# A Mamba-2 layer on one core: the scan's products and transposes in one insert per pair, x and z of a pair change places

## The chip, the core and the metric

The kernel runs on one core of a Trainium2 chip. The metric is the device time of one execution in microseconds (us). Before the change three runs took 1293.35, 1293.44 and 1298.07 us; the median is 1293.44 us.

## What is computed

One layer of a streaming encoder on 512 tokens with 2048 channels: RMSNorm, a Mamba-2 mixer, a residual add and a final RMSNorm, all in float32.

```
hn  = rmsnorm(x, ln_g)
proj = hn @ w_in                       # 2048 -> z 4096, x 4096, B 8*128, C 8*128, dt 64
xbc = silu(causal_depthwise_conv(x|B|C, 4 taps))
dt  = softplus(dt + dt_bias);  a = -exp(a_log)
y   = ssd_scan(xs * dt, dt * a, B, C)  # 64 heads of 64 channels, 8 groups share B and C, state 128
y   = y + d_skip * xs
y   = rmsnorm(y * silu(z), norm_g)
out = rmsnorm(x + y @ w_out, final_g)
```

## The kernel before

**Float32 from two halves.** Every weight tile is split into a rounded part `hi` (a CAST on ScalarE, ACT, line 87) and a rest `lo` (a subtraction on VectorE, DVE, line 88). A product is then three matmuls per 128x128 block: hi times x hi, hi times x lo, lo times x hi (lines 635 to 637).

**Stages.** After a short first part (B, C, x and z of the first two units, called plain) come 36 pairs, then the output projection. The 4096 inner channels are 32 units of 128 channels (two heads). A pair is the projection of two tiles of 128 channels: x and z of one unit, or, once per group of four units, B and C of the next group. The order of the pairs is x,z of unit 4g, of 4g+1, then B,C of group g+1, then x,z of 4g+2 and of 4g+3.

**A pair.** `pair` (line 639) computes both tiles with seven products in place of eight (a Strassen form over the two halves of the 2048 inputs and the two halves of the tokens). Each product is 24 matmuls, that is 4 steps of 6 matmuls, and a pair is 28 steps (`QS`). The products of a pair are R11 (steps 0 to 4), T1 (4 to 8), the previous pair's T4 (8 to 12), T2 (12 to 16), R22 (16 to 20), R21 (20 to 24) and T3 (24 to 28); a pair's own T4 is done in the next pair (`last`). PSUM tile `R` holds T1 and R22, `S` holds R11, T2 and T3, `mm` the sum that T4 ends. One of the two tiles (`zq`, lines 679 and 683) is complete when T3 is, at step 28; the other when T4 is, at step 40, which is step 12 of the next pair. Before the change x is the later one (line 398) and z the earlier one (line 689).

**The weights of a pair** come in four loads on SP's queue (line 81: `ra`, `rb`, two `rc`), T1 and T3 are made by accumulating DMAs on GpSimd (POOL, line 598), T2 and T4 by additions on DVE (line 604). `q_events` says at which step each is loaded, formed and split.

**The scan of a unit** is six functions, hung on steps after the start of the unit's pair by the table in line 713:

- `u_load`: three DMAs on SP, of which `csb` (line 440, 512 KB, one buffer) is the decay row spread over all partitions.
- `u_decay`: twelve ACT instructions (lines 456 to 458) and one more (459) that make the decay mask `m` from `csb`, and a DVE multiplication (461).
- `u_xt`: four transposes on TensorE (PE, line 473) of `xs`, the convolved x after its SiLU (line 394), then `xd` and `xw` on DVE.
- `u_state` (PE line 488, then the split `sts`) and `u_yd` (PE lines 502 and 506, then DVE 509).
- `u_yo`: three matmuls (lines 518 to 520), DVE 521 to 523, the store of y to `yscr` (SP, line 524), and the sum of squares (ACT 528, DVE 529).

A group also has `g_cb` (lines 433 and 434, the products of B and C) and `g_bt` (line 416, transposes of B).

**What sets the order.** PE, SP and POOL run their instructions in the order in which the program gives them: `run(step)` calls what the tables put on a step ahead of that step's matmuls. DVE and ACT get their order from a scheduler that works on priorities; `urgent()` raises one. All queues run in order: an instruction that waits holds up those behind it. SP runs ahead of PE until a transfer's buffer or data isn't there; the store of y is where it mostly stands.

Of the kernel before, what the change touches and what calls it, by code (L numbers as in the profile page):

```python
# [10 lines left out]
F32 = mybir.dt.float32  # L11
F32R = mybir.dt.float32r
AF = mybir.ActivationFunctionType
ALU = mybir.AluOpType
# [3 lines left out]
P = 128  # L18
L = 512
# [7 lines left out]
UPG = 4  # L27
NU = G * UPG
# [6 lines left out]
def mamba_layer(ctx: ExitStack, tc: tile.TileContext, d: dict, out: bass.AP):  # L35
    nc = tc.nc
    V, S, T, Q = nc.vector, nc.scalar, nc.tensor, nc.gpsimd
# [3 lines left out]
    urgent = tc.high_priority  # L41
# [9 lines left out]
    sp = ph1.enter_context(tc.tile_pool(name="ssd", bufs=1))  # L51
# [52 lines left out]
    yscr = [dram.tile([P, UPG, L], F32, name=f"yscr{g}") for g in range(G)]  # L104
# [4 lines left out]
    NPL = 8  # L109
    seq = [(("B", 0), ("C", 0))]  # L110
# [2 lines left out]
            seq.append((("B", u // UPG + 1), ("C", u // UPG + 1)))  # L113
        seq.append((("x", u), ("z", u)))
    plain = [s for pair in (seq[0], seq[1], seq[2], seq[3]) for s in pair]
    quads = seq[NPL // 2:]
    tile_of = {"z": 0, "x": 32, "B": 64, "C": 72}
    QS = 28
    at = {s: i * KT for i, s in enumerate(plain)}
# [49 lines left out]
    xr = sp.tile([P, L + 48], F32, name="xr")  # L169
# [15 lines left out]
    sx = const.tile([P, L], F32, name="sx")  # L185
# [94 lines left out]
    rbc = const.tile([P, L], F32, name="rbc")  # L280
# [104 lines left out]
    def conv_silu(t, name):  # L385

        ca = sp.tile([P, L], F32, name=name, bufs=2)
        V.tensor_scalar(out=ca, in0=xr[:, 3:L + 3], scalar1=convw[:, t, 3:4], scalar2=convb[:, t:t + 1],
                        op0=ALU.mult, op1=ALU.add)
        for k in range(3):  # L390
            V.scalar_tensor_tensor(out=ca, in0=xr[:, k:k + L], scalar=convw[:, t, k:k + 1], in1=ca,
                                   op0=ALU.mult, op1=ALU.add)
        with urgent():
            S.activation(ca, ca, AF.Silu)
        return ca

    def normed(ps):
        V.tensor_tensor(out=xr[:, 3:L + 3], in0=ps, in1=rbc, op=ALU.mult)  # L398
# [9 lines left out]
    un = [dict() for _ in range(NU)]  # L408

    def g_b(g):  # L410
        gr[g]["B"] = conv_silu(32 + g, "bc")
# [10 lines left out]
    def g_c(g):  # L422
        gr[g]["C"] = conv_silu(40 + g, "bc")
        gr[g]["Cs"] = split(gr[g]["C"][:, LH:L], [P, LH], "cst", 2)
# [70 lines left out]
    def u_yd(u):  # L495

        pyd = ps_yd.tile([P, 2, 2 * P], F32, name="yd")
        xs, x, m = un[u]["xs"], un[u]["xd"], un[u]["m"]
        for i in range(2):
            for hh in range(2):  # L500
                r = slice(hh * HD, hh * HD + HD)
                T.matmul(pyd[r, i, :], x[:, 2 * i, hh, :], m[:, i, hh::4, :],  # L502
                         start=i == 0, stop=False, skip_group_check=True)
            for hh in range(2):
                r = slice(hh * HD, hh * HD + HD)
                T.matmul(pyd[r, i, P:2 * P], x[:, 2 * i + 1, hh, :], m[:, i, 2 + hh, :],
                         start=False, stop=i == 1, skip_group_check=True)
        y = xs
        V.scalar_tensor_tensor(out=y, in0=xs, scalar=dskip[:, u:u + 1], in1=pyd.rearrange("p c l -> p (c l)"),
                               op0=ALU.mult, op1=ALU.add)  # L510
        un[u]["y"] = y

    def u_yo(u):

        y, ecs, z = un[u]["y"], un[u]["ecs"], un[u]["z"]
        pyo = un[u]["pyo"].rearrange("p b l -> p (b l)")[:, 0:2 * P]
        (ah, al), (bh, bl) = un[u]["sts"], gr[u // UPG]["Cs"]
        T.matmul(pyo, ah, bh, start=True, stop=False)
        T.matmul(pyo, ah, bl, start=False, stop=False)
        T.matmul(pyo, al, bh, start=False, stop=True)  # L520
        V.tensor_tensor(out=ecs, in0=pyo, in1=ecs, op=ALU.mult)
        V.tensor_tensor(out=y[:, 2 * P:L], in0=y[:, 2 * P:L], in1=ecs, op=ALU.add)
        V.tensor_tensor(out=y, in0=y, in1=z, op=ALU.mult)
        nc.sync.dma_start(yscr[u // UPG][:, u % UPG, :], y)
        if u == 0:
            S.activation(sx, y, AF.Square)
        else:
            S.activation(z, y, AF.Square)
            V.tensor_tensor(out=sx, in0=sx, in1=z, op=ALU.add)

# [95 lines left out]
    def product(ps, w, f, first, step):  # L628

        for k in range(KH):  # L630
# [5 lines left out]
            T.matmul(ps, hi[:, k, :], al, start=False, stop=False, skip_group_check=True)  # L636
            T.matmul(ps, lo[:, k, :], ah, start=False, stop=k == KH - 1, skip_group_check=True)  # L637

    def pair(n, prev):

        b = NPL * KT + n * QS
        (kp, ip), (kq, iq) = quads[n]
        s_, r_ = ps_s.tile([P, L], F32, name="S")[:, lo_], ps_q.tile([P, LH], F32, name="R")
        sn = sp.tile([P, 2, LH], F32, name="sn")
        zq = xr[:, 3:L + 3] if kq == "C" else sp.tile([P, L], F32, name="z", bufs=2)
        W = lambda f: lambda: qs[n, f]
        A = ps_mm.tile([P, L], F32, name="mm")

        def first(step):
            product(s_, W("R11"), 11, True, step)  # L650
            with urgent():
                S.copy(out=A[:, lo_], in_=s_)

        def second(step):
            product(r_, W("T1"), 1, True, step)
            with urgent():
                S.copy(out=sn[:, 1, :], in_=r_)

        if prev:
            first(b)  # L660
            second(b + 4)
            prev(b + 8)
        else:
            second(b)
            first(b + 4)
            for i in range(8, 12):
                run(b + i)
        def third(step):
            product(r_, W("R22"), 4, False, step)

        def fourth(step):
            product(s_, W("T2"), 2, False, step)
            with urgent():
                S.copy(out=sn[:, 0, :], in_=s_)

        for f, step in zip((fourth, third) if prev else (third, fourth), (b + 12, b + 16)):
            f(step)
        with urgent():
            V.tensor_tensor(out=zq[:, lo_], in0=r_, in1=sn[:, 0, :], op=ALU.add)
        product(A[:, lo_], W("R21"), 12, False, b + 20)  # L680
        product(s_, W("T3"), 3, False, b + 24)
        with urgent():
            V.tensor_tensor(out=zq[:, hi_], in0=s_, in1=sn[:, 1, :], op=ALU.add)
            S.copy(out=A[:, hi_], in_=s_)
        if kq == "C":
            V.scalar_tensor_tensor(out=zq, in0=zq, scalar=-1.0, in1=rbc, op0=ALU.mult, op1=ALU.mult)
            g_c(iq)
        else:
            V.tensor_tensor(out=zq, in0=zq, in1=rbc, op=ALU.mult)
            S.activation(zq, zq, AF.Silu, scale=-1.0)  # L690
            un[iq]["z"] = zq

        def last(step):
            product(A[:, hi_], W("T4"), 22, False, step)
            with urgent():
                normed(A)
            (g_b if kp == "B" else u_x)(ip)
            qs.pop(n)
        return last

# [3 lines left out]
    def add(step, f, *a):  # L704
        ev.setdefault(step, []).append((f, a))

    for g in range(1, G):
        add(at["B", g] + (30 if ("B", g) in plain else 93), g_bt, g)
        for i in range(2):
            add(at["x", 4 * g] + 28, g_cb, g, i)  # L710
    ramp = [[66, 71, 63, 75, 87, 92], [56, 65, 50, 68, 86, 92]]
    for u in range(NU):
        w = ramp[u] if u < len(ramp) else [28, 42, 56, 65, 65, 71]
        for o, f in zip(w, (u_load, u_decay, u_xt, u_state, u_yd, u_yo)):
            add(at["x", u] + o, f, u)
    for n in range(len(quads)):
        q_events(n, NPL * KT + n * QS, n == len(quads) - 1, 0 if n else 14, lone=not n)
    for i in range(4):
# [3 lines left out]
    def run(step):  # L722
        for f, a in ev.pop(step, ()):
            f(*a)

    def finish(n, ps):
        kind, i = plain[n]
        if kind == "z":
            z = sp.tile([P, L], F32, name="z", bufs=2)
            V.tensor_tensor(out=z, in0=ps, in1=rbc, op=ALU.mult)  # L730
            S.activation(z, z, AF.Silu)
            un[i]["z"] = z
        else:
            normed(ps)
            {"B": g_b, "C": g_c, "x": u_x}[kind](i)
# [53 lines left out]
    for n in range(2, NPL):  # L789
        ps = None  # L790
        for k in range(KT):
# [3 lines left out]
            if ps is None:  # L795
                ps = (ps_mm.tile([P, L], F32, name="mm") if n % 2 == 0 else
                      ps_s.tile([P, L], F32, name="S"))
# [8 lines left out]
    for n in range(len(quads)):  # L806
        prev = pair(n, prev)
# [177 lines left out]
    first = [ps_s.tile([P, L], F32, name="S"), ps_mm.tile([P, L], F32, name="mm")]  # L985
# [9 lines left out]
    op = ctx.enter_context(tc.tile_pool(name="op", bufs=1, side="right"))  # L995
# [5 lines left out]
    for kb, blk in enumerate(blocks[:-1]):  # L1001
# [8 lines left out]
        for s, pairs in blk:  # L1010
            ps = [None] * NC
# [38 lines left out]
    for t in range(NC):  # L1050
        ss = fp.tile([P, 4], F32, name="ss", bufs=2)
        for s in range(4):
            ps = ps_o.tile([P, L], F32, name="mm")
            for i in range(2):
# [6 lines left out]
                            op=ALU.mult)  # L1061
# [7 lines left out]
        for i in range(n):  # L1069
            c = slice(i * (DM // n), (i + 1) * (DM // n))  # L1070
# [41 lines left out]
```

## Time and profile before

| | |
|---|---|
| median of the runs | 1293.44 us |
| the profiled execution | 1295.7 us |
| its span, first to last instruction | 1294.0 us |
| PE busy | 1252.1 us (97%) |
| DVE busy | 1084.3 us (84%) |
| ACT busy | 826.6 us (64%) |
| mean granted TensorE clock | 0.991 |

A matmul row in the timeline has its start and its length; the lengths overlap, so what a matmul costs is the distance to the next start. "[1.54 <-DVE lo L88]" behind a row says that the engine was idle 1.54 us before it, until DVE's instruction of line 88 that writes `lo` had ended. The PEclk column is the share of the full clock (2.4 GHz) that was granted.

### The profile page before, as it was taken

What the parts mean: (1) busy time and instruction counts of PE and PEld (TensorE: products, weight loads), DVE (VectorE), ACT (ScalarE), POOL (GpSimd) and SP (SyncE); (2) the same over time, 40 slices, a digit from 0 to 9 for tenths busy, and PEclk for the clock granted to TensorE, in tenths of its full rate; (3) what the DMA queues carried; (4) which work ended last, traced back from release to release, by engine and by line L of the source; (5) the groups of instructions that cost most, each with busy time, mean ns of one, the idle gap of its engine ahead of it and who ended that gap; (6) DMA issues with size and microseconds to landing.
All of it is one profiled execution on the core that took longest, in us unless ns stands there. A gap on an engine that the chain in (4) does not pass through costs nothing.

```text
span 1294.0 us, 24519 instructions
## 1 busy us (share of the span) xinstructions
PE 1252.1 (97%) x9932; PEld 1192.9 (92%) x9932; DVE 1084.3 (84%) x1449; ACT 826.6 (64%) x1357; POOL 77.5 (6%) x99
## 2 busy tenths in 40 slices
PE   8989899999999999999999999999999899999997
PEld 8989899999999999999999999999988899899885
DVE  5796988988989898998889899889857877887865
ACT  7667667677666757767685867778666445434433
POOL 0000001010000101010100001000000000000000
PEclk9989999999999999999999999999999999999999
DMA  9546657585676667667667677766637576647612
GB/s 356 179 141 172 162 161 174 143 215 142 192 197 174 159 169 183 164 176 199 162 161 195 151 188 171 212 155 154 185 105 258 146 199 199 197 119 229 183 57 98
DMA packets 70194, 225.90 MB, mean 175 GB/s; under 512 B 8384, under 2 KB 12800, under 8 KB 69952
## 3 DMA queue, kind: packets, MB, share of 16 engines
q1 hardware_dynamic: 56688, 176.34, 40.2%
q0 software_dynamic: 12672, 46.14, 22.1%
q8 instruction: 78, 1.28, 0.4%
q10 hardware_dynamic: 720, 1.84, 0.4%
q14 instruction: 36, 0.29, 0.1%
HBM read 211.52 MB, written 12.78 MB: 173 GB/s over the span
## 4 chain that ended last, share of the span: by engine, by line
PE 74%; DVE 11%; DMA 7%; issue 4%; ACT 3%; SPq 0%; POOL 0%; DVEq 0%; ACTq 0%; POOLq 0%
PE S L637 7%; PE S L635 7%; PE S L636 7%; PE mm L635 5%; PE mm L636 4%; PE R L635 4%; PE mm L637 4%; PE R L636 4%; PE R L637 4%; DVE lo L88 3%; PE mm L929 3%; PE mm L931 3%; PE mm L930 3%; PE yd L502 2%; PE mm L867 2%
## 5 line engine op out<-in xcount | busy, mean ns | idle before, releaser
L87 ACT CAST hi<-ra 128x1024 fp32r<-128x1024 f32 x150 | 154.7, 1046 | 159.5 <-DVE ra L604 72.9
L88 DVE TENSOR_TENSOR lo<-ra,hi 128x1024 fp32r<-128x1024 f32 x150 | 181.3, 1221 | 24.2 <-ACT hi L87 24.1
L635 PE MATMUL mm<-xh,hi 128*128 128x256 f32 x576 | 163.6, 284 | 0.0
L637 PE MATMUL mm<-xh,lo 128*128 128x256 f32 x576 | 160.6, 279 | 0.6 <-DVE lo L88 0.6
L636 PE MATMUL mm<-xl,hi 128*128 128x256 f32 x576 | 160.4, 278 | 0.0
L637 PE MATMUL R<-s,lo 128*128 128x256 f32 x576 | 160.3, 278 | 0.1
L635 PE MATMUL R<-s,hi 128*128 128x256 f32 x576 | 160.2, 278 | 0.0
L636 PE MATMUL R<-s,hi 128*128 128x256 f32 x576 | 160.2, 278 | 0.0
L88 DVE TENSOR_TENSOR lo<-rc,hi 128x1024 fp32r<-128x1024 f32 x94 | 114.9, 1223 | 28.5 <-ACT hi L87 28.1
L87 ACT CAST hi<-rc 128x1024 fp32r<-128x1024 f32 x94 | 98.4, 1047 | 50.8 <-issue 29.1
L604 DVE TENSOR_TENSOR ra<-ra,rc 128x1024 f32<-128x1024 f32 x88 | 107.7, 1224 | 13.3 <-DMA rc<-in_wi 11.8
L635 PEld LDWEIGHTS mm<-xh,hi 128*128 128x128 f32 x576 | 108.1, 188 | 5.2 <-issue 5.0
L637 PEld LDWEIGHTS mm<-xh,lo 128*128 128x128 f32 x576 | 109.2, 190 | 0.8 <-DVE lo L88 0.8
L637 PEld LDWEIGHTS R<-s,lo 128*128 128x128 f32 x576 | 109.1, 189 | 0.3 <-DVE lo L88 0.3
L635 PEld LDWEIGHTS R<-s,hi 128*128 128x128 f32 x576 | 108.2, 188 | 0.0
L636 PEld LDWEIGHTS mm<-xl,hi 128*128 128x128 f32 x576 | 108.2, 188 | 0.0
L636 PEld LDWEIGHTS R<-s,hi 128*128 128x128 f32 x576 | 108.1, 188 | 0.0
L637 PE MATMUL S<-xh,lo 128*128 128x256 f32 x288 | 83.5, 290 | 5.6 <-DVE lo L88 5.6
L635 PE MATMUL S<-xh,h1h 128*128 128x256 f32 x288 | 83.4, 290 | 1.0 <-DVE xr L398 1.0
L635 PE MATMUL S<-xh,hi 128*128 128x256 f32 x288 | 81.3, 282 | 2.2 <-ACT xh L577 1.3
L636 PE MATMUL S<-xl,hi 128*128 128x256 f32 x288 | 81.2, 282 | 0.7 <-DVE xl L578 0.7
L636 PE MATMUL S<-xl,h1h 128*128 128x256 f32 x288 | 80.8, 280 | 0.0
(452 smaller groups left out, 3940.8 us busy)
## 6 DMA issues: line engine op xcount, KB each, us to landing
rc<-in_wi SPq DMA_DIRECT2D x76, 512.0 KB, 5.9
ra<-in_wi SPq DMA_DIRECT2D x42, 512.0 KB, 6.2
rb<-in_wi SPq DMA_DIRECT2D x40, 512.0 KB, 6.9
ra<-in_wi POOLq DMA_DIRECT2D x36, 512.0 KB, 6.3
rb<-in_wi POOLq DMA_DIRECT2D x36, 512.0 KB, 5.9
csb<-cscr SPq DMA_DIRECT2D x32, 512.0 KB, 8.0
ra<-in_wo SPq DMA_DIRECT2D x26, 512.0 KB, 5.4
yscr<-xs SPq DMA_DIRECT2D x32, 256.0 KB, 2.6
```

The costliest lines, as they stand in the source:

```text
L87: S.copy(out=hi, in_=raw)
L88: V.tensor_tensor(out=lo, in0=raw, in1=hi, op=ALU.subtract)
L502: T.matmul(pyd[r, i, :], x[:, 2 * i, hh, :], m[:, i, hh::4, :], start=i == 0, stop=False, skip_group_check=True)
L604: V.tensor_tensor(out=raw, in0=raw, in1=qs[n][other], op=ALU.add)
L635: T.matmul(ps, hi[:, k, :], ah, start=first and k == 0, stop=False, skip_group_check=True)
L636: T.matmul(ps, hi[:, k, :], al, start=False, stop=False, skip_group_check=True)
L637: T.matmul(ps, lo[:, k, :], ah, start=False, stop=k == KH - 1, skip_group_check=True)
L867: T.matmul(ps[:, t, :], yh[:, k, tt], hi[:, k, :], start=st, stop=False, skip_group_check=True)
L929: T.matmul(ps, yh, hi, start=first and k == 0, stop=False)
L930: T.matmul(ps, yh, lo, start=False, stop=False)
L931: T.matmul(ps, yl, hi, start=False, stop=last and k == 1)
```

## The change

Three things change together.

- In the pairs, z takes the late place and x the early one: a pair is (z, x) where it was (x, z). x is normalised with the negative sign in one instruction and convolved at step 28, as C was; z is gated (`gate`) at step 40.
- The steps of a unit: load 42 (was 28), decay 54 (42), transposes 44 (56), state and yd 72 (65), yo 78 (71). Since a pair is 28 steps, 72 is 44 of the next unit: the products of a unit and the transposes of the next unit's x are one insert. `g_cb` and `g_bt` of a group move together to step 34 of the group's first pair. The first two units keep their steps; the last has its own.
- y times the gate is written over z and no longer over xs, and the squares go to the PSUM tile `yd` of the unit, so the early x doesn't wait for the store.

```diff
-    quads = seq[NPL // 2:]
+    quads = [pair if pair[0][0] == "B" else pair[::-1] for pair in seq[NPL // 2:]]
...
-        V.tensor_tensor(out=y, in0=y, in1=z, op=ALU.mult)
-        nc.sync.dma_start(yscr[u // UPG][:, u % UPG, :], y)
+        V.tensor_tensor(out=z, in0=y, in1=z, op=ALU.mult)
+        nc.sync.dma_start(yscr[u // UPG][:, u % UPG, :], z)
         if u == 0:
-            S.activation(sx, y, AF.Square)
+            S.activation(sx, z, AF.Square)
         else:
-            S.activation(z, y, AF.Square)
-            V.tensor_tensor(out=sx, in0=sx, in1=z, op=ALU.add)
+            y2 = un[u]["pyd"]
+            S.activation(y2, z, AF.Square)
+            V.tensor_tensor(out=sx, in0=sx, in1=y2, op=ALU.add)
...
+    def gate(u, ps, first=False):
+        z = sp.tile([P, L], F32, name="z", bufs=2)
+        with urgent() if first else ExitStack():
+            V.tensor_tensor(out=z, in0=ps, in1=rbc, op=ALU.mult)
+        S.activation(z, z, AF.Silu)
+        un[u]["z"] = z
...
-        zq = xr[:, 3:L + 3] if kq == "C" else sp.tile([P, L], F32, name="z", bufs=2)
+        zq = xr[:, 3:L + 3]
...
-        if kq == "C":
-            V.scalar_tensor_tensor(out=zq, in0=zq, scalar=-1.0, in1=rbc, op0=ALU.mult, op1=ALU.mult)
-            g_c(iq)
-        else:
-            V.tensor_tensor(out=zq, in0=zq, in1=rbc, op=ALU.mult)
-            S.activation(zq, zq, AF.Silu, scale=-1.0)
-            un[iq]["z"] = zq
+        V.scalar_tensor_tensor(out=zq, in0=zq, scalar=-1.0, in1=rbc, op0=ALU.mult, op1=ALU.mult)
+        (g_c if kq == "C" else u_x)(iq)
...
-            with urgent():
-                normed(A)
-            (g_b if kp == "B" else u_x)(ip)
+            if kp == "B":
+                with urgent():
+                    normed(A)
+                g_b(ip)
+            else:
+                gate(ip, A, True)
...
-        add(at["B", g] + (30 if ("B", g) in plain else 93), g_bt, g)
         for i in range(2):
-            add(at["x", 4 * g] + 28, g_cb, g, i)
-    ramp = [[66, 71, 63, 75, 87, 92], [56, 65, 50, 68, 86, 92]]
+            add(at["x", 4 * g] + 34, g_cb, g, i)
+        add(at["x", 4 * g] + 34, g_bt, g)
+    steps = {0: [66, 71, 63, 75, 87, 92], 1: [56, 65, 50, 68, 86, 92], NU - 1: [36, 46, 44, 65, 65, 71]}
     for u in range(NU):
-        w = ramp[u] if u < len(ramp) else [28, 42, 56, 65, 65, 71]
-        for o, f in zip(w, (u_load, u_decay, u_xt, u_state, u_yd, u_yo)):
-            add(at["x", u] + o, f, u)
+        w = steps.get(u, [42, 54, 44, 72, 72, 78])
+        for f in (3, 4, 5, 0, 2, 1):
+            add(at["x", u] + w[f], (u_load, u_decay, u_xt, u_state, u_yd, u_yo)[f], u)
```

The order of the instructions on three engines, at the places that the prediction speaks of. Names before the arrow are what is written, behind it what is read; line numbers are each kernel's own.

PE before: a unit's products in the middle of T4 (on `mm`), and the next unit's transposes at the start of the next pair, between T3 and R11 (both on `S`):

```order
L637 MATMUL mm<-xh,lo 128x256
L488 MATMUL yo<-xw,bt 128x128 x2
L502 MATMUL yd<-m,xd 64x256 x2
L506 MATMUL yd<-m,xd 64x128 x2
L502 MATMUL yd<-m,xd 64x256 x2
L506 MATMUL yd<-m,xd 64x128 x2
L635 MATMUL mm<-xh,hi 128x256
...
L637 MATMUL S<-xh,lo 128x256
L473 MATMUL tr<-ident,xs 128x128 x4
L635 MATMUL S<-xh,h1h 128x256
```

And with the change, between T2 on `S` and R22 on `R`:

```order
L638 MATMUL S<-s_833,lo 128x256
L488 MATMUL yo<-xw,bt 128x128 x2
L502 MATMUL yd<-m,xd 64x256 x2
L506 MATMUL yd<-m,xd 64x128 x2
L502 MATMUL yd<-m,xd 64x256 x2
L506 MATMUL yd<-m,xd 64x128 x2
L473 MATMUL tr<-ident,xs 128x128 x4
L636 MATMUL R<-s_638,hi 128x256
```

Of the 32 units' transposes 22 now stand behind the products of the unit before; those of the first unit behind a B,C pair stand alone, and each group's `g_cb` and `g_bt` are an insert of their own. Counting the stretches on PE, up to the output projection, that hold transposes of x or B, `g_cb` or the products of units from 2 on, there were 61 and are 45.

DVE before, in a pair of units, from the split of the state to T3's `lo` (`lo<-rb`):

```order
L404 TENSOR_TENSOR stsl<-yo,stsh 128x128
L509 SCALAR_TENSOR_TENSOR xs<-xs,par,yd 128x512
L398 TENSOR_TENSOR xr<-mm,rbc 128x512
L388 TENSOR_SCALAR xs<-xr,par 128x512
L88 TENSOR_TENSOR lo<-rc,hi 128x1024
L391 SCALAR_TENSOR_TENSOR xs<-xr,par,xs 128x512
L521 TENSOR_TENSOR ecs<-yo,ecs 128x256
...
L523 TENSOR_TENSOR xs<-xs,z 128x512
L461 TENSOR_TENSOR m<-m,cbm 128x1536
L88 TENSOR_TENSOR lo<-rb,hi 128x1024
```

With the change:

```order
L404 TENSOR_TENSOR stsl<-yo,stsh 128x128
L509 SCALAR_TENSOR_TENSOR xs<-xs,par,yd 128x512
L476 TENSOR_TENSOR xd<-tr,dt 128x512
L88 TENSOR_TENSOR lo<-rb,hi 128x1024
L479 TENSOR_TENSOR xw<-xd,win 128x256
L687 TENSOR_TENSOR xr<-R,sn 128x256
L88 TENSOR_TENSOR lo<-ra,hi 128x1024
L521 TENSOR_TENSOR ecs<-yo,ecs 128x256
```

T3's `lo` is now the fourth instruction from the state's split, ahead of the convolution and of the decay mask's multiplication.

ACT with the change, in the last pair of a group (units 4g+3), from the copy that R11's end allows:

```order
L660 COPY mm<-S 128x256
L456 ACTIVATE m<-csb,cs 128x128
L457 ACTIVATE m<-csb,cs 128x128
L458 ACT_TABLE_LOAD
L458 ACTIVATE m<-csb,nwl 128x128
L665 COPY sn<-R 128x256
L87 CAST hi<-rc 128x1024
L456 ACTIVATE m<-csb,cs 128x128
L394 ACT_TABLE_LOAD
L394 ACTIVATE xs<-xs 128x512
L644 ACTIVATE z<-z 128x512
L87 CAST hi<-rc 128x1024
```

Before, the decay began at the same place but the SiLU of x stood behind all of it and behind T3's cast. The SiLU of x now stands in the middle of the decay, between two table loads; this order is the same in all six such pairs behind a B,C pair, and the whole program has 85 table loads where it had 71. On SP the four loads of a pair (`rc`, `ra`, `rc`, `rb`) stood between the store of y and `csb`; now `csb` stands directly behind the store.

## Rows read from the trace of the kernel before

**Rows 1.** The page's first part: busy time, share of the span, instructions.

```profile
PE 1252.1 (97%) x9932; PEld 1192.9 (92%) x9932; DVE 1084.3 (84%) x1449; ACT 826.6 (64%) x1357; POOL 77.5 (6%) x99
```

**Rows 2.** Windows, start of the pairs and steady pairs; length, engines' busy, PEclk, DMA share, GB/s.

```profile
126.00:170.00 44.00, 38.65 (x298) 36.68 (x297) 39.05 (x50) 27.71 (x45) 2.58 (x3) 0.92 0.61 164
195.00:920.00 725.00, 720.18 (x6245) 701.94 (x6245) 649.77 (x834) 516.49 (x887) 55.82 (x65) 1.00 0.68 175
```

**Rows 3.** Waits on PE, 195 to 920 us: total, times, longest.

```profile
PE S L637 <- DVE lo L88: 4.8, 8, 1.5
```

**Rows 4.** Timeline of PE at one such wait, in T3: start, length.

```profile
499.62 0.28 PE L636 MATMUL S<-xl,hi 128*128 128x256 f32 x1
501.43 0.39 PE L637 MATMUL S<-xh,lo 128*128 128x256 f32 x1 [1.54 <-DVE lo L88]
```

**Rows 5.** Timeline of DVE ahead of that wait.

```profile
497.50 1.75 DVE L461 TENSOR_TENSOR m<-m,cbm 128x1536 f32<-128x1536 f32 x1
...
499.83 0.42 DVE L679 TENSOR_TENSOR z<-R,sn 128x256 f32<-128x256 f32 x1
500.16 1.21 DVE L88 TENSOR_TENSOR lo<-rb,hi 128x1024 fp32r<-128x1024 f32 x1
```

**Rows 6.** Timeline of PE: transposes alone; behind `g_cb`; end of a unit's products.

```profile
503.93 0.28 PE L637 MATMUL S<-xh,lo 128*128 128x256 f32 x1
504.05 0.60 PE L473 MATMUL tr<-ident,xs 128*128 128x128 f32 x4
...
504.61 0.28 PE L636 MATMUL S<-xl,h1h 128*128 128x256 f32 x1
...
527.63 0.60 PE L473 MATMUL tr<-ident,xs 128*128 128x128 f32 x4
527.99 0.37 PE L635 MATMUL S<-xh,h1h 128*128 128x256 f32 x1
...
558.26 0.39 PE L506 MATMUL yd<-m,xd 128*64 128x128 f32 x4
558.58 0.39 PE L635 MATMUL mm<-xh,hi 128*128 128x256 f32 x1
```

**Rows 7.** Timeline of ACT, the decay's begin in a pair of unit 4g+3.

```profile
488.95 0.40 ACT L456 ACTIVATE m<-csb,cs 128x128 f32<-128x128 f32 x1 [0.71 <-DMA csb<-cscr]
...
489.65 1.28 ACT L458 ACT_TABLE_LOAD   x1
490.94 0.40 ACT L458 ACTIVATE m<-csb,nwl 128x128 f32<-128x128 f32 x1
...
492.46 0.40 ACT L456 ACTIVATE m<-csb,cs 128x128 f32<-128x128 f32 x1
...
500.56 0.63 ACT L394 ACTIVATE xs<-xs 128x512 f32<-128x512 f32 x1
```

**Rows 8.** Timeline of SP's queue: `csb` behind a store, and behind four loads.

```profile
149.02 0.33 SPq L524 DMA_DIRECT2D yscr<-xs  x1
149.39 0.43 SPq L440 DMA_DIRECT2D csb<-cscr  x1
...
479.74 0.70 SPq L440 DMA_DIRECT2D csb<-cscr  x1
```

**Rows 9.** Tile `csb`, issue to landing: 140 to 170 us (two), then 195 to 920 (26).

```profile
DMA to landing us min/median/max: 4.7/4.7/4.8
...
DMA to landing us min/median/max: 4.8/8.4/9.7
```

**Rows 10.** Waits on PE, 126 to 170 us, first and last of six; clock in two windows there.

```profile
PE S L635 <- ACT xh L577: 1.3, 1, 1.3
...
PE mm L637 <- DVE lo L88: 0.6, 1, 0.6
...
145.00:149.00 4.00, 3.51 (x18) 3.54 (x19) 4.00 (x9) 2.75 (x4) 0.00 (x0) 0.57 0.40 79
163.00:170.00 7.00, 5.33 (x30) 4.93 (x30) 4.95 (x5) 3.29 (x4) 0.00 (x0) 0.76 0.58 198
```

More of the change, by code (lines that the diff above doesn't have):

```diff
@@ L510, in u_yd @@
                                op0=ALU.mult, op1=ALU.add)
-        un[u]["y"] = y
+        un[u]["y"], un[u]["pyd"] = y, pyd.rearrange("p c l -> p (c l)")
     def u_yo(u):
@@ L728, in finish @@
         if kind == "z":
[L729 to L732, printed above, removed]
+            gate(i, ps)
         else:
```

## The prediction

> **What bounds the kernel now.** First the page's busy shares [rows 1]: PE is at work for 97% of the span, DVE for 84%, ACT for 64%. An average over stages says little, so next the windows [rows 2]: in the steady pairs, 195 to 920 us, PE is busy for 720.2 of 725 us at full clock and DVE for 90%; from 126 to 170 us, where the pairs begin, PE is busy for 38.7 of 44 us and the clock is 0.92. So the kernel is as long as PE's list plus the holes in it. The holes of the steady pairs are one line in the waits of PE [rows 3]: eight times, for 4.8 us in all, PE waits in T3 for the `lo` half of T3's weights. The timeline shows one [rows 4]: two matmul starts lie 1.81 us apart, where neighbours lie 0.11 apart; that is 1.70 us lost for a wait shown as 1.54. Eight of them, each 0.16 longer than shown, are 4.8 + 1.3 = 6.1 us. Why the `lo` is late shows on DVE [rows 5]: it starts at 500.16, behind the decay mask's multiplication (1.75 us) and what follows it, when its product was already running.
>
> The profiled execution took 1295.7 us (span 1294.0), 2.3 us above the median of the three runs, 1293.44. I make the sum against the execution and take 2.3 us off at the end.
>
> **a. T3's waits: -6.1 us.** The new DVE order has T3's `lo` ahead of the convolution and the mask. Times from the pair's start, with 0.113 us per matmul and so 0.68 per step: the insert begins at step 16, 10.9 us; products and transposes take 2.1 + 0.36 (below), so PE is through at 13.3. DVE then does `xd`, 128x512 and so half of the 1.21 us that a 128x1024 operation takes [rows 5], 0.6 us, and `lo`, 1.2; with a quarter of a microsecond for the semaphore it ends at 15.4. T3 begins after eight more steps and `yo`, at 13.3 + 5.4 + 0.3 = 19.0. So there are 3.6 us of slack. What is late next is T4's `lo`, which comes after T3's end, the `S` addition and 1.2 us: about 24 us against its use at step 36, 27.3; the other splits have more. Bounds: all 6.1 gone, or none gone if DVE, 90% busy, is late elsewhere. I take 6.1.
>
> **b. Fewer inserts: -1.5 us.** Transposes alone cost [rows 6] 504.61 - 503.93 = 0.68 us, less two ordinary matmuls, 0.45. Behind `g_cb` they take 527.99 - 527.63 = 0.36, and the last stretch of a unit's products is followed by the same changeover. So joining saves 0.09 us. It would save 0.19 if the products' own last gap (558.58 - 558.26 = 0.32 where 0.22 is usual) shrank too. Joined 22 times, and `g_cb` with `g_bt` taken out on their own: 61 stretches become 45. 16 x 0.09 = 1.5, at most 16 x 0.19 = 3.0. I take 1.5, from the row of a transposes' stretch that really stands behind products. The transposes themselves are all still there.
>
> **c. The early decay in the last pair of a group: +3.0 us.** Here the change adds a wait. `u_load` issues three DMAs on SP, and moving it past the four weight loads puts `csb` directly behind the store of y, which waits for unit 4g+1's y. Six times (the pairs of unit 4g+3 behind a B,C pair) ACT begins the decay after R11's copy, at step 4, 3.3 us. That instruction waits for `csb`, and behind it in the queue stand the copy of `R`, the cast for R22, and now the SiLU of x, for which PE's transposes wait at step 16, 10.9 us; behind these stands R22. The stretch [rows 7]: from the decay's start to the second one, with a table load, copy and cast, 492.46 - 488.95 = 3.51 us; then 0.40, a table load of 1.28, SiLU 0.63: 5.8 us, and 0.1 to PE. So `csb` may land at 5.0 us without cost. When is it issued? `yo` is at step 22 of the pair before, ends at about 17.4 us; DVE's five operations behind it (two of 128x256 at 0.33 from start to start, two of 128x1024 and one of 128x512, by rows 5: 0.7 + 2.4 + 0.6) end y some 0.2 us before the next pair starts, at 21.5; SP issues `csb` 0.37 us after a store [rows 8]; so it lands at 0.2 us plus its landing time. That time is 4.7 us where it stood directly behind a store, and 8.4 in the middle of 26, up to 9.7, where it stood behind four loads of 512 KB [rows 8, 9]. Cost of one pair: nothing at 4.7, 0.6 at 5.4, 3.6 at 8.4, 4.9 at 9.7. The nearest row is the first, but T3's accumulating DMA of 512 KB will be under way; I take 5.3, 0.5 us, six times. Bounds 0 and 29.
>
> The 14 further table loads are 14 x 1.28 = 18 us of ACT, at 64% busy; the two that matter are in the 5.8 us above, the others stand in ACT's idle time. In rows 7 the load takes 1.28 us and the next instruction starts 0.01 us after it. The Trainium skill, "ScalarE: Activation LUTs", section "What ACT_TABLE_LOAD costs", counts a drain of about 1.38 us on top, 2.66 us per switch, which speaks against a change that adds switches; by that figure the six pairs would be 2 x 1.38 us longer each and the sum 16.6 us higher. The trace doesn't agree with the drain: 0.01 us stands there.
>
> **d. The start of the pairs: 0.** Before, six waits of 1.3 to 0.6 us and two stretches at half clock cost 5.3 + 4 x 0.43 + 7 x 0.24 = 8.7 us there [rows 10]. In the new order the last forms of x are done earlier, which takes two waits away, and T3's cast of the second pair stands ahead of the decay, which takes two more. Against that, x now needs the buffer `xr`, still read by the convolution of C, so `R` is freed late, about 2 us; and unit 2's decay repeats c, with the first `csb`, for 3 to 4 us. Bounds: 8.7 gained, or one more wait of 4.9 and a half-clock stretch of 1.7, 6.6 lost. I take 0, as the sums of waits that go and come are near each other.
>
> **e. The rest: -0.5.** A wait for `lo` of 0.5 us at the start of the output projection has its DVE work moved forward. Edits at nothing: z and x normalised in each other's place (the same DVE operations), squares into PSUM, one ACT and one DVE operation as before, both behind work on which nobody waits. The store of y moves from step 15 to 22, but its readers come much later; past it, the four loads of a pair now start as soon as their buffers are free, so DVE's waits for `rc` can only shrink.
>
> **The sum:** -6.1 - 1.5 + 3.0 + 0 - 0.5 = -5.1, so 1290.6 for the execution profiled and **1288.3 us** for the median. Half a per cent, about what a measurement of this kernel can tell from no change, is 6.5 us: faster means below 1287.0, slower above 1299.9.
>
> **Rivals.**
>
> 1. *As forecast, T3's waits go and c costs little*: 1283 to 1294, with b up to 3.0 and d between -4 and +4. 0.45.
> 2. *`csb` lands late*, place c, in ACT's queue. At the median of 8.4 us, 6 x 3.6 = 21.6 in place of 3.0, +18.6: 1307. Slower than before by half a per cent needs 1299.9 - 1288.3 + 3.0 = 14.6 us in c, 2.4 per pair, a landing of 7.2 us. For it: 26 landings of 8.4. Against it: each of those stood behind four loads, which now come after. 0.17.
> 3. *The start becomes smooth too and c costs nothing*: -3.0 for c, -5 for d: 1280. For it: the new order lifts four of six waits and with them the half-clock stretches. 0.22.
> 4. *The waits only move*: DVE is 90% busy, and another `lo` is late instead; a falls away, b and c balance: 1292. Against it: DVE's slack of 3 us at each split. 0.14.
> 5. *ACT's further table loads all lie on the path*: 14 x 1.28 = 17.9 us more, 1306. Nothing in rows 7 speaks for it but the place of two loads. The rule on the drain, cited above from the Trainium skill's "ScalarE: Activation LUTs", would work the same way. 0.02.
>
> That the change doesn't do what it says is excluded by the order of PE.
>
> **Numbers.** Of case 1 two fifths lie below 1287.0, 0.18; with case 3 faster is 0.40. Slower: cases 2 and 5, less 0.02 of case 2 that ends below 1299.9: 0.17. The rest, 0.43, is within half a per cent. The range from 1279 to 1302 leaves out most of case 2 and case 5 (0.14) and the lower edge of case 3 (0.04). The likeliest case's own range is 1283 to 1294.
>
> **What would show it.** a: the line of rows 3 is gone or below 1 us. b: a product insert with transposes takes 2.46 us. c: PE's transposes of x wait for ACT's SiLU in six places, and the landing of `csb` there is below 6 us; if it is above 7, case 2 holds. d: the clock from 126 to 170 us and the waits there. The prediction is wrong if new waits of PE for DVE's `lo` stand in the steady pairs, or if the execution is outside 1281 to 1304.

## The result, and the profile after

The changed kernel took **1309.06 us** (median of 6 runs, 1305.56 to 1311.43) beside 1293.39 us of the kernel before (6 runs, 1290.54 to 1298.07): a ratio of 1.0113, 95% interval 1.0093 to 1.0133. It is slower by 1.1%, outside the forecast's range. The profiled execution is the fastest of the six, 1305.56 us; its span is 1303.8 us, 9.8 us longer than the 1294.0 of the kernel before. The other five had a lower mean granted clock (0.980 to 0.984, where the profiled one had 0.985); how much of the 3.5 us between it and the median that explains is not shown, since two runs at 0.984 took 1307.76 and 1310.80 us.

The busy shares answer to [rows 1]: PE works 8.6 us less than before, in a longer span, ACT 20.4 us more.

```profile
PE 1243.5 (95%) x9932; PEld 1185.1 (91%) x9932; DVE 1081.8 (83%) x1449; ACT 847.0 (65%) x1371; POOL 77.8 (6%) x99
```

The windows answer to [rows 2]. In the steady pairs PE's busy time has fallen from 720.2 to 705.2 of 725 us: holes of 20 us where 5 us were.

```profile
126.00:170.00 44.00, 36.95 (x287) 35.56 (x287) 37.47 (x49) 28.04 (x43) 3.59 (x4) 0.92 0.62 157
195.00:920.00 725.00, 705.21 (x6174) 688.22 (x6173) 641.16 (x827) 525.87 (x884) 55.08 (x64) 0.99 0.66 173
```

The waits of PE, 195 to 920 us, answer to [rows 3]. T3's waits for `lo` are gone. One line stands in their place: the transposes wait for ACT's SiLU of x.

```profile
PE tr L473 <- ACT xs L394: 19.8, 6, 4.4
```

The six stand where the forecast looked for them, in the pairs of unit 4g+3, and each is 3.1 to 4.5 us from start to start, 20.8 us in all. One of them on PE; in full pace the transposes would have started 0.11 us after the matmul at 496.82:

```profile
496.82 0.28 PE L638 MATMUL S<-s,lo 128*128 128x256 f32 x1
500.08 1.11 PE L473 MATMUL tr<-ident,xs 128*128 128x128 f32 x4 [2.99 <-ACT xs L394]
```

ACT, the same pair, which begins at 486.05. The decay is next at 490, stands until `csb` has landed at 494.17, and the SiLU of x ends 5.86 us later, at 500.03:

```profile
489.82 0.37 ACT L660 COPY mm<-S 128x256 f32<-128x256 f32 x1
494.17 0.40 ACT L456 ACTIVATE m<-csb,cs 128x128 f32<-128x128 f32 x1 [3.98 <-DMA csb<-cscr]
...
494.88 1.28 ACT L458 ACT_TABLE_LOAD   x1
...
498.11 1.28 ACT L394 ACT_TABLE_LOAD   x1
499.40 0.63 ACT L394 ACTIVATE xs<-xs 128x512 f32<-128x512 f32 x1
```

SP's queue, the same pair, then the answer for this one `csb`: issued 1.62 us after the pair's begin, landed 6.5 us later (1.60 to 1.62 and 6.4 to 7.9 in all six).

```profile
487.29 0.33 SPq L524 DMA_DIRECT2D yscr<-z  x1
487.67 0.45 SPq L440 DMA_DIRECT2D csb<-cscr  x1
```

```profile
DMA to landing us min/median/max: 6.5/6.5/6.5
```

Behind four of the six waits the granted clock falls to the lower level, 1.2 GHz, for a stretch of 3.41 us. Some 0.5 us of it lies in the hole itself; in the rest, from the transposes on, matmuls start 0.213 us apart where 0.113 is usual, which costs 1.4 us. The windows round them show it in the column ahead of the DMA share, at 1.00 elsewhere in the pairs:

```profile
274.00:279.00 5.00, 4.14 (x24) 4.14 (x25) 3.12 (x4) 4.97 (x8) 0.00 (x0) 0.66 0.65 226
500.00:504.00 4.00, 3.92 (x23) 3.92 (x24) 2.48 (x3) 3.98 (x7) 0.00 (x0) 0.62 0.83 271
612.00:617.00 5.00, 4.24 (x25) 4.25 (x26) 3.12 (x4) 4.96 (x9) 0.00 (x0) 0.66 0.70 236
725.00:729.00 4.00, 3.56 (x20) 3.57 (x21) 2.13 (x3) 3.98 (x7) 0.00 (x0) 0.59 0.78 264
```

A further hole stands at the start of the output projection. PE needs the buffer `mm`, which the normalisation of the last z frees; timelines of PE, DVE, ACT and SP:

```profile
943.96 0.39 PE L934 MATMUL S<-hi,h1l 128*128 128x512 f32 x1
947.17 0.80 PE L932 MATMUL mm<-hi,h1h 128*128 128x512 f32 x1 [2.82 <-DVE z L643]
```

```profile
943.84 1.23 DVE L88 TENSOR_TENSOR lo<-rb,hi 128x1024 fp32r<-128x1024 f32 x1 [1.73 <-ACT hi L87]
944.98 1.53 DVE L391 SCALAR_TENSOR_TENSOR xs<-xr,par,xs 128x512 f32<-128x512 f32 x2
946.43 0.68 DVE L643 TENSOR_TENSOR z<-mm,rbc 128x512 f32<-128x512 f32 x1
```

```profile
942.75 1.05 ACT L87 CAST hi<-rb 128x1024 fp32r<-128x1024 f32 x1 [3.36 <-DMA rb<-in_wo]
```

```profile
936.43 0.33 SPq L524 DMA_DIRECT2D yscr<-z  x1
936.86 0.37 SPq L81 DMA_DIRECT2D rb<-in_wo  x1
```

The z stands on DVE behind the `lo` of an output weight piece, whose load SP issues behind the store of y. It costs 3.0 us from start to start, where such matmuls usually lie 0.23 apart, and a half-clock stretch that costs 1.7 us follows.

**Where the 9.8 us are**, between the two profiled executions. From the start to the first pair (121.3 us before, 120.4 now) -0.9; to 173 us +1.2; the 33 pairs from there (736.8 and 744.2 us) +7.4; the output projection +2.1. Within the pairs: T3's waits -8.2 (the eight listed ones -6.1; the rest is a longer distance from start to start behind each, and nine distances of 0.22 us that wait for `lo` too but are too short for the list of waits); the six new waits +20.8; their half-clock stretches 4 x 1.4 = +5.5. That is +18.1 where +7.4 was measured. So 10.7 us were won elsewhere: about 1.5 in the inserts, as forecast, and most of the rest in a way that the forecast did not have, a second pace of PE.

**The second pace.** In the kernel before, some 2500 of the 5544 distances from the start of one weight matmul of these pairs to the next are 117.7 ns and most others 113.3, in long stretches, both at a granted clock of 1.00; in the changed kernel some 315 are slow. Over all of these distances that makes 9.6 us. A change of pace on PE's timeline of the kernel before: 14 matmuls in 1.59 us, one in 0.22, then 20 in 2.36:

```profile
299.07 0.28 PE L635 MATMUL mm<-xh,hi 128*128 128x256 f32 x1
...
300.66 0.39 PE L637 MATMUL S<-xh,lo 128*128 128x256 f32 x1
300.88 0.28 PE L635 MATMUL S<-xh,hi 128*128 128x256 f32 x1
...
303.24 0.28 PE L637 MATMUL S<-xh,lo 128*128 128x256 f32 x1
```

What switches it is taken up by experiments 4, 5 and 7. (The recorded expectations have 2623 slow ones, 117.6 and 4.35 ns; the difference of the two paces is 4.4 ns.)

### The profile page after: what moved, and what is told of

It is laid out like the page before. It is cut to its first block, busy times and chain, and to the rows that moved or that the text cites. A ratio compares the mean times of both kernels' runs of the same rounds, so it can differ in the third digit from the quotient of the medians.

```text
span 1303.8 us, 24525 instructions
## 1 busy us (share of the span) xinstructions
PE 1243.5 (95%) x9932; PEld 1185.1 (91%) x9932; DVE 1081.8 (83%) x1449; ACT 847.0 (65%) x1371; POOL 77.8 (6%) x99
## 4 chain that ended last, share of the span: by engine, by line
PE 59%; DVE 16%; DMA 11%; ACT 7%; issue 6%; SPq 0%; DVEq 0%; ACTq 0%
PE S L636 4%; PE S L638 4%; PE S L637 4%; PE R L636 4%; PE R L637 4%; PE R L638 4%; DMA csb<-cscr 3%; DVE lo L88 3%; PE mm L636 3%; PE mm L637 3%; PE mm L638 3%; PE mm L932 3%; PE mm L934 3%; PE mm L933 3%; ACT hi L87 3%
## 5 line engine op out<-in xcount | busy, mean ns | idle before, releaser
L636 PE MATMUL R<-s,hi 128*128 128x256 f32 x576 | 166.9, 290 | 2.3 <-DVE xr L687 2.3
L637 PE MATMUL R<-s,hi 128*128 128x256 f32 x576 | 162.5, 282 | 0.0
L636 PE MATMUL mm<-xh,hi 128*128 128x256 f32 x576 | 159.3, 277 | 0.0
L636 PEld LDWEIGHTS R<-s,hi 128*128 128x128 f32 x576 | 111.9, 194 | 3.6 <-DVE xr L687 2.5
L637 PEld LDWEIGHTS R<-s,hi 128*128 128x128 f32 x576 | 111.7, 194 | 0.0
L636 PE MATMUL S<-xh,h1h 128*128 128x256 f32 x288 | 79.7, 277 | 0.0
L638 PE MATMUL S<-s,lo 128*128 128x256 f32 x288 | 79.7, 277 | 0.0
L638 PE MATMUL S<-xh,h1l 128*128 128x256 f32 x288 | 79.6, 277 | 0.0
L636 PE MATMUL S<-s,hi 128*128 128x256 f32 x288 | 79.6, 276 | 0.0
```

The costliest lines, as they stand in the source:

```text
L636: T.matmul(ps, hi[:, k, :], ah, start=first and k == 0, stop=False, skip_group_check=True)
```

## The experiments

Each was timed beside runs of the kernel before on the same chip; ratios are to those.

**1. `csb` ahead of the store.** For the first unit behind a B,C pair the three loads are issued 28 steps earlier.

```diff
-        w = steps.get(u, [42, 54, 44, 72, 72, 78])
+        w = steps.get(u, [14 if u % UPG == 2 else 42, 54, 44, 72, 72, 78])
```

> The changed kernel, but the csb of the first unit behind a B,C pair (units 2, 6, 10, ...) is issued 28 steps earlier, ahead of the pair's weight loads and of the store of y. Theory A (in six pairs ACT starts this unit's decay early and stands there until csb has landed, and the SiLU of x, for which PE's transposes wait, stands behind): csb then lands before the pair of unit 4g+3 begins, the six waits of 3.1 to 4.5 us (20.8 us from start to start) go, and with them the four half-clock stretches behind them (4 x 1.7 us): 1309.1 - 27.6 = 1281.5, at most 1287. Rival B (DVE and ACT have no room there, the stall only moves): ACT now stands for csb one pair earlier, in front of the SiLU of B and of casts, and PE waits there instead: 1303 to 1311.

1277.55 us (4 runs, 1277.24 to 1278.34), ratio 0.9859 [0.9831, 0.9886]. No wait of PE is left from 195 to 905 us. On SP `csb` now follows the store of unit 4g and no longer that of 4g+1, a whole pair earlier:

```profile
453.81 0.33 SPq L524 DMA_DIRECT2D yscr<-z  x1
454.23 0.43 SPq L440 DMA_DIRECT2D csb<-cscr  x1
```

**2. The SiLU ahead of the decay.** `csb` stays late; ACT can't begin the decay first.

```diff
         m = sp.tile([P, 2, 6, P], F32, name="m")
+        if u % UPG == 2:
+            S.copy(out=m[:, :, :, 0:1], in_=un[u]["xs"][:, 0:12].rearrange("p (c b l) -> p c b l", c=2, l=1))
```

> The changed kernel, with a copy of 12 columns of x's SiLU into the decay's buffer ahead of the decay, in the units 2, 6, 10, ...: ACT can't begin the decay before the SiLU of x; csb is issued as late as in the changed kernel, and lands as late. The copied numbers are overwritten by the decay. Theory A (late csb costs only because the SiLU stands behind it in ACT's queue): the six waits of PE's transposes go though csb still lands 6 us after its issue, 1309.1 - 27.6 = 1281.5, 1279 to 1285. Rival C (x itself is late there, by DVE's convolution or its own inputs): the transposes wait as before, 1303 to 1311. Rival D (the decay, now later, makes the mask's product late for PE's products one pair on): a new wait of 1 to 3 us in six places, 1287 to 1299.

1277.37 us (4 runs, 1275.13 to 1278.76), ratio 0.9855 [0.9825, 0.9884]. `csb` of the same unit lands as late as in the changed kernel, and it costs nothing. Its landing, the window of the pairs, and ACT's timeline:

```profile
DMA to landing us min/median/max: 6.8/6.8/6.8
```

```profile
195.00:900.00 705.00, 704.99 (x6233) 688.56 (x6232) 645.64 (x833) 515.29 (x885) 54.95 (x64) 1.00 0.67 179
```

```profile
484.35 0.64 ACT L394 ACTIVATE xs<-xs 128x512 f32<-128x512 f32 x1 [0.52 <-DVE xs L391]
...
485.50 0.19 ACT L452 COPY m<-xs 128x12 f32<-128x12 f32 x1
485.72 0.40 ACT L458 ACTIVATE m<-csb,cs 128x128 f32<-128x128 f32 x1
```

The SiLU no longer stands within the decay, which also saves 13 of the 85 table loads; experiment 1 still has 81 and reaches the same time. So it takes both: a late `csb`, and an instruction that waits for it standing in front of one that PE waits for. Either repair takes the loss away. The gain, 31.5 us of the changed kernel's median, is 4 us more than expected; between the profiled executions, from which the expectation was made, it is 28.2 and 28.8 us.

**3. Both repairs.** In addition the second piece of the output weights is loaded ahead of the store of y.

```diff
-    add(END - 4, get_out, 1, "rb")
+    add(END - 7, get_out, 1, "rb")
```

> The same as the kernel with the SiLU ahead of the decay, and in the last pair the load of the output weights' second piece (rb) stands ahead of the store of y on SP, three steps earlier. Theory: the one wait of 2.8 us at the start of the output projection (3.1 from start to start), for the normalisation of the last z on DVE, comes from DVE standing in front of it for the lo of that piece, whose load is issued behind the store; it goes, and the half-clock stretch of 1.7 us behind it too: 4.8 us less than the kernel with the SiLU ahead of the decay, so 1276.7 by theory A. Rival: z is late for another reason (the convolution of the last x, also ahead of it on DVE): the same time as that kernel within 1 us.

1272.96 us (4 runs, 1271.97 to 1277.35), ratio 0.9829 [0.9797, 0.9861]; 4.4 us below experiment 2, where 4.8 were expected, though the single runs of the two overlap. The wait for z is gone, but the size agrees for another reason: two waits of 0.9 and 1.0 us have come in, for the copy of S and for the `lo` of the last T4, on PE's timeline at

```profile
909.92 0.39 PE L936 MATMUL mm<-hi,h1l 128*128 128x512 f32 x1
911.02 0.38 PE L638 MATMUL mm<-xh,hi 128*128 128x256 f32 x1 [0.72 <-ACT mm L694]
911.25 0.28 PE L639 MATMUL mm<-xl,hi 128*128 128x256 f32 x1
912.37 0.38 PE L640 MATMUL mm<-xh,lo 128*128 128x256 f32 x1 [0.84 <-DVE lo L88]
```

Against the 2.3 us of z in experiment 2 only 0.4 is won there, and 1.7 for the clock. In these two profiles the output projection's pace counts for more: in experiment 2 a slow stretch began in the last pair, at 900 us, and 1213 of the 1356 distances between matmuls of 256 columns that follow were slow, here 159, which is 4.7 us; other waits there, longer here, take 4 us back. That was no part of the theory. So the wait for z is shown to go; that its going is worth 4.4 us is not shown.

**4. The transposes apart.** Both repairs, with the inserts split again: transposes two steps (12 matmuls) behind the products.

```diff
-        w = steps.get(u, [42, 54, 44, 72, 72, 78])
+        w = steps.get(u, [42, 54, 46, 72, 72, 78])
```

> The kernel with both repairs, but the transposes of a unit come two steps (12 matmuls) behind the products of the unit before instead of directly behind, so that an insert is split into two again, as before the change; x and z keep their changed places. The changed kernel's PE takes 113.3 ns from matmul to matmul nearly everywhere, the kernel before took 117.6 ns for 2623 of 5543 of them, at the same granted clock: 11 us. Theory P1 (the slow pace comes in behind PE's waits for lo in T3, which the new order of DVE has removed): the pace stays at 113.3 and only the 22 further changeovers cost 0.06 to 0.09 each: 1.3 to 2.0 us more than the kernel with both repairs. Theory P2 (it comes in behind an insert that ends with a unit's products): the slow pace is back for a third to a half of the matmuls, 8 to 12 us more.

1273.34 us (4 runs, 1271.65 to 1276.94), ratio 0.9821 [0.9788, 0.9854]: no slower than experiment 3 that can be measured in the medians. The traces are finer: the 33 pairs take 718.3 us here, 716.4 and 717.2 in experiments 3 and 8, and with the pace taken out 1.2 us more than in either. Joining the inserts is by itself worth that, 0.06 for each. The trace tells more: of the 28 inserts that now end with products 13 put PE into the slow pace, and behind all 13 the transposes ended it two steps later, so that only some 140 matmuls were slow. (The 17 in the expectations of experiments 5 and 7 is too high: behind the other 15 inserts only the first four distances are longer.) So P2's switch is there, and P1's forecast that the pace stays at 113.3 fell; the price of P2 was set too high, since the way back was so near.

**5. The transposes first.** Both repairs, joint inserts, but transposes ahead of the products.

```diff
+    for u in range(3, NU):
+        add(at["x", u] + 44, u_xt, u)
...
-        for f in (3, 4, 5, 0, 2, 1):
+        for f in (3, 4, 5, 0, 2, 1) if u < 3 else (3, 4, 5, 0, 1):
```

> The kernel with both repairs (1272.96 us), but within the joint insert the transposes of the next unit stand ahead of the products instead of behind them, from unit 3 on, so that the insert ends with the products. As many inserts and changeovers as before, no wait for lo in T3. In the kernel with the transposes apart, 17 of 28 inserts that end with products put PE from 113.3 to 117.6 ns per matmul, and all 17 came back behind the transposes two steps later. Theory P2 (the slow pace begins behind an insert that ends with products and lasts until one that ends with transposes): with no such transposes behind, from a third to two thirds of the 5544 matmuls are slow, 1850 to 3700 x 4.35 ns: 8 to 16 us more, 1281 to 1289. Theory P1 (the slow pace is no matter of the inserts' order): 1272 to 1275. If the transposes, now 2.1 us earlier, wait for the SiLU of x, that shows as a wait of PE for ACT and is taken off.

1306.08 us (5 runs, 1304.29 to 1308.72), ratio 1.0100 [1.0067, 1.0134], slower than both theories said, for the reason that the expectation set aside:

```profile
PE tr L475 <- ACT xs L394: 22.1, 20, 1.9
```

The products' 2.1 us are what hides the SiLU of x. That is what "transposes behind" is worth in this change. Some 1020 matmuls were slow (4.5 us), fewer than P2 said; 7 of the 26 inserts that now end with products and were entered in the fast pace began the slow one. The waits blur the test of the pace.

**6. The kernel before with T3's split earlier.** Term a by itself.

```diff
-                        (17, q_split, ("T3",)), (23 if last else 29, q_split, ("T4",))):
+                        (13 if n else 17, q_split, ("T3",)), (23 if last else 29, q_split, ("T4",))):
```

> The kernel before, unchanged but for T3's split, which is put into the order of the work four steps earlier (from the second pair on), so that DVE makes T3's lo ahead of the decay mask's multiplication. Two separate inserts, x and z in their old places. Theory (term a by itself): the eight waits of T3 and the four small ones (6.1 + 1.3 us) go, and of the ways into the slow pace the six behind those waits, while those behind the products stay: 1295.2 - 7.4 = 1287.8 and some microseconds less, 1281 to 1288. Rival P1 (only T3's waits bring the slow pace in): all of its 11 us go too, 1276. Rival (DVE, 90% busy, is late elsewhere instead): 1292 to 1298.

1310.35 us (4 runs, 1309.01 to 1314.14), ratio 1.0139 [1.0100, 1.0177]: a miss. PE's waits, 195 to 920 us, first two lines:

```profile
PE mm L635 <- ACT mm L684: 8.9, 4, 3.6
PE S L637 <- DVE lo L88: 4.8, 8, 1.3
```

T3's waits are as many as before, in other places, and new ones for ACT's copy have come. DVE, for which ACT waits there, stands more for the loads of `rc` (29.3 us in 21 waits, 11.8 in 12 in the kernel before). That is the third rival's mechanism, at a higher price than it gave. So this edit does not give a by itself; whether another would is not shown. The gain of a in the change came with its whole new order of DVE.

**7. The transposes eight steps behind.** Experiment 4 with 52 in place of 46, so that transposes stand 48 matmuls behind the products.

> The kernel with both repairs, with the transposes of a unit eight steps (48 matmuls) behind the products, at the start of T3, instead of two steps as in the kernel with the transposes apart. No wait of PE for them is expected, as x's SiLU is ready. Theory P2 (an insert that ends with products puts PE into the pace of 117.6 ns in some 17 of 28 cases, and the next transposes bring it back): the slow stretches become four times as long, about 17 x 48 = 820 slow matmuls where two steps gave 170, 820 x 4.35 ns = 3.6 us, so 1272.96 + 3.6 + 0.4 = 1277. Theory P3 (the pace changes at inserts of any kind, by chance): the number of slow matmuls does not follow the distance, and the time may be anything from 1272 to 1283. If DVE is late with T3's lo, whose place is now ahead of the transposes' xd, nothing of this shows but new waits of T3.

1276.08 us (4 runs, 1274.66 to 1278.13), ratio 0.9857 [0.9832, 0.9883]. Over the 33 pairs it takes 720.9 us, 3.7 more than experiment 8 on the same chip. Some 660 matmuls were slow: 540 behind products, four times experiment 4, and one further stretch of 118. Of 27 inserts that end with products and were entered in the fast pace 12 began the slow one, and behind each of these 12 the transposes ended it. One of them on PE's timeline: 12 matmuls ahead of the products in 1.36 us, 30 behind them in 3.53, 24 behind the transposes in 2.72, that is 113.3, 117.7 and 113.3 ns each.

```profile
545.52 0.28 PE L638 MATMUL S<-s,hi 128*128 128x256 f32 x1
...
546.88 0.28 PE L638 MATMUL S<-s,hi 128*128 128x256 f32 x1
```

```profile
548.24 0.60 PE L490 MATMUL yo<-xw,bt 128*128 128x128 f32 x4
...
550.69 0.28 PE L638 MATMUL R<-s,hi 128*128 128x256 f32 x1
...
554.22 0.28 PE L638 MATMUL mm<-xh,hi 128*128 128x256 f32 x1
...
556.34 0.60 PE L475 MATMUL tr<-ident,xs 128*128 128x128 f32 x4
```

```profile
557.02 0.28 PE L640 MATMUL S<-xh,lo 128*128 128x256 f32 x1
...
559.74 0.28 PE L640 MATMUL S<-xh,h1l 128*128 128x256 f32 x1
```

P2 holds and P3 falls: these slow stretches last from the products to the transposes, at either distance. The further stretch does not fit P2: it began at 706.8 us in T3, at a distance of 0.17 us behind a matmul whose `lo` had come 0.1 us before it, and ended behind products. The 12 are all products of even units, and so are the 13 in experiment 4. Inserts of `yo` alone never changed the pace (none of 28 here).

**8. Both repairs again.** The kernel of experiment 3, unchanged.

> The kernel with both repairs once more, in five rounds, beside the kernel before on the same chip: 1272.96 us was its median, 0.983 of before. Theory A: the same within 3 us, no wait of PE for ACT's SiLU from 170 us on, nearly all matmuls of the pairs at 113.3 ns. If the pace is a matter of chance from run to run, its profile shows stretches at 117.6 ns this time.

1274.65 us (4 runs, 1273.22 to 1276.06), ratio 0.9841 [0.9819, 0.9862]. The window of the pairs has no hole:

```profile
195.00:900.00 705.00, 705.00 (x6238) 688.46 (x6237) 646.28 (x834) 515.75 (x887) 54.95 (x64) 1.00 0.68 179
```

166 matmuls were slow, behind one of 22 joint inserts. So the change with two repairs beats both kernels: 1.6% below before, 34 us below the change as it was made.

## Why the prediction was wrong

The failing step is **c**, whose six pairs were priced at 0.5 us each and cost 3.1 to 4.5. Its place, its chain and its slack were right. The slack can be read off all six: "`csb` may land at 5.0 us without cost", counted from the pair's start, and the decay began 8.04 to 9.51 us after the pair's start, for losses of 3.08 to 4.54; the difference is 4.97 or 4.98 in each. The ACT stretch from decay to SiLU, put at 5.8 us, took 5.86. Two inputs were wrong; summed over the six pairs the first is worth 8.5 us and the second 9.0, which with the 3.0 forecast is nearly all of the 20.8.

- *When `csb` is issued*: said 0.2 us after the pair's start, measured 1.60 to 1.62. (By the forecast's own terms y ends at 21.1, which is 0.4 and not 0.2 us ahead of 21.5; that slip is small beside this.) DVE's operations behind `yo` were counted from the rows of the old order. In the new one R11's `lo` slipped ahead of the first of them, which starts 1.5 us after the end of `yo` at 482.14; the operations from there on take what was forecast:

```profile
482.50 1.23 DVE L88 TENSOR_TENSOR lo<-ra,hi 128x1024 fp32r<-128x1024 f32 x1 [0.17 <-ACT hi L87]
483.64 0.42 DVE L521 TENSOR_TENSOR ecs<-yo,ecs 128x256 f32<-128x256 f32 x1
...
486.58 0.69 DVE L523 TENSOR_TENSOR z<-xs,z 128x512 f32<-128x512 f32 x1
```

  The new DVE order that stood beside the forecast shows that `lo<-ra` as the row ahead of `ecs`: this could have been counted.
- *How long it takes to land*: 5.3 was taken, near the 4.7 of a `csb` directly behind a store [rows 9]; it took 6.4 to 7.9. T3's accumulating load of 512 KB is under way then, from POOL at 486.37. In the six pairs `csb` is issued 1.2 to 1.3 us behind that load; the others that stand behind a store in these pairs come 2.2 to 3.8 us behind it and land after 4.2 to 6.4 us. That fits the load as the cause, but it was not tested. The forecast's sign for case 2, a landing above 7 us, held in one pair of six, since it counted on the early issue.

Also left out of c: the clock. A hole of 3 to 4.5 us in PE brought a half-clock stretch in four of six places, 1.4 us each (the expectations of experiments 1 and 2 have 1.7). The working had such stretches only in d.

Point by point:

- **a**, -6.1: all eight waits are gone, as forecast, and with them 2 us of short delays that the list of waits does not show. Experiment 6 shows that its reason was too narrow: having `lo` ahead of the mask does not do it in the old order.
- **b**, -1.5: a joint insert takes 547.03 - 544.31 = 2.72 us, less two ordinary matmuls 2.49, where 2.46 was forecast; apart, the products take 2.10 and the transposes 0.45. That is 0.06 saved for each where the working had 0.09, and experiment 4 finds the same in its trace.

```profile
544.31 0.28 PE L638 MATMUL S<-s,lo 128*128 128x256 f32 x1
544.42 0.60 PE L488 MATMUL yo<-xw,bt 128*128 128x128 f32 x4
...
546.82 0.37 PE L636 MATMUL R<-s,hi 128*128 128x256 f32 x1
547.03 0.28 PE L637 MATMUL R<-s,hi 128*128 128x256 f32 x1
```

- **d**, 0: +1.2 from 121 to 173 us. The wait of `R` for `xr`, put at 2 us, is there with 2.3, and that of unit 2's transposes, put at 3 to 4, with 2.6.
- **e**, -0.5: the old wait is gone, but the one for z took its place, 3.0 and 1.7 for the clock. The store's move from step 15 to 22 was called free because "its readers come much later". What counted was a load queued behind it on SP, which the change had not touched.
- *The pace* was missing: -9.6 us. The kernel before had it all along, in matmuls that start 0.12 us apart instead of 0.11, at full granted clock; the sum took 0.113 for all.

Of the rivals, 2 (`csb` lands late, 1307) named the mechanism, and the median came within 2.1 us of its time. That is half a coincidence: its 21.6 us for six waits is close to the 20.8 measured, while the clock (+5.5), the wait for z (+4.7) and the pace (-9.6), none of which it had, nearly cancel. "Each of those stood behind four loads, which now come after" was the argument that gave it only 0.17; it weighed the landing alone, and the issue time moved as well. Rival 5 fell: experiment 1 keeps 10 of the 14 further table loads and loses nothing to them.

## What to carry to other kernels

When a change lets a scheduler start an off-path stage earlier, look at what stands behind its first instruction in an in-order queue: if that instruction waits, everything behind it waits too, though nobody needs its own result yet. Compute such a slack to the microsecond, and then compute its inputs (issue time, landing) from the new order and not from rows of the old one, since a slack that is right is worth nothing beside an issue time that is off by one queue entry. A transfer that comes to stand behind a moved store is part of the change too, and a hole in PE should be priced with the half-clock stretch that may follow: here that came with four of six holes of 3 to 4.5 us.

## What the runs showed that was not expected

PE has two paces at the same granted clock of 1.00: 128x256 matmuls that each load new weights start 113.3 or 117.7 ns apart, which is 4% of a stretch that consists of them. Two things mostly began the slow one. One is an insert that ends with a unit's products, whose weights have 64 columns: 13 of the 14 even units and none of the 14 odd ones in experiment 4, 12 even and no odd one in experiment 7. The six inserts of the changed kernel that still end with products belong to odd units, and none of them began it. The other is a `lo` that comes just in time: in the kernel before 7 of the 12 slow stretches of the 33 pairs began in T3 at a distance of 0.22 us behind a matmul whose `lo` had ended 0.06 us before it, and 5 behind products; T3's eight longer waits began none. So P1 of experiment 4 was right in part, for the short waits. Where the transposes stand directly behind the products it hardly ever began (none of 22 inserts in experiments 1 and 3 each, 1 in experiment 8, 3 in experiment 2); the two slow stretches of the changed kernel began behind two of the four half-clock stretches. In experiments 4 and 7 it ended behind transposes (13 of 13 and 12 of 12). Why a few small matmuls set the pace of the hundreds behind them, and what the parity of the unit has to do with it, stays open. It shows in start-to-start distances alone, in no listed wait and in no clock.
